# A decoder block on one core: the forget gate's two small products, both blocks of positions at a time

## The chip, the core and the metric

The kernel runs on one core of a Trainium2 chip. A core has TensorE (PE in the rows of the profile; its weight loads are shown as PEld), VectorE (DVE), ScalarE (ACT), GpSimd (POOL) and SyncE (SP), which here issues all DMA transfers. Each engine works through its own queue of instructions in order, and semaphores order the engines among each other. Matmul results go to PSUM, which has 8 banks; a bank holds 128 partitions of 512 float32 values. The metric is device time in microseconds (us) of one execution; several runs are given, and their median.

## The reference

One layer on 2048 positions of width 1024: an RMS norm, one input projection whose columns feed two token mixers (gated linear attention in chunks, and a short gated convolution), an output projection with residual, a SwiGLU feed-forward part with residual, and a last norm. All in float32. What the change touches is the forget gate of the attention, a product with a narrow matrix of rank 16 and a second product that widens it again:

```python
h = rmsnorm(x, norm1_g[l])
proj = h @ w_in[l]
p_q, p_k, p_v, p_g, p_a, c_b, c_c, c_h = jnp.split(proj, splits, axis=-1)   # p_a: 16 columns
gate_logits = (p_a @ w_gate_up[l] + b_gate[l]).astype(jnp.float32)          # 16 -> 256
log_a = (jax.nn.log_sigmoid(gate_logits) / GATE_NORMALIZER).reshape(bsz, seq, GLA_HEADS, GLA_DK)
o = gla_chunked(q, k, v, log_a)     # needs cumulative sums of log_a inside each chunk
```

## The kernel before

Features lie on partitions and positions along the free axis: a tile is 128 features by 512 positions (`PB`). The 2048 positions are four blocks of 512, worked on as two halves of two blocks. Every large product is made with operands split into a high and a low part (`split`: ScalarE copies the high part, VectorE subtracts to get the low part), three matmuls for each step of 128 (lines 328 to 330 in `product_step`: high·high, high·low, low·high).

A large product of a half is a `unit`: a 2 x 2 block product (two halves of the contraction, two blocks of positions) made with seven block products instead of four. The seven operands on the side of the positions are `B11` (features 0 to 511, first block), `B21` (features 512 to 1023, first block), `B22` (features 512 to 1023, second block) and the combinations `T1` = B12 - B11, `T2` = B22 - T1, `T3` = B22 - B12 and `T4` = B21 - T2 (the last made from T2 in place). `B12` itself, the second block's features 0 to 511, isn't kept as a full set of seven; it is `B11` + `T1`. Each operand is a list of four slices of 128 features, each with a high and a low part. For the first half `build_first` makes them on the fly: GpSimd subtracts (line 288), ScalarE and VectorE split (lines 146 and 147); the first unit's products run meanwhile. For the second half they were made earlier (`h1_ahead`), stored to DRAM and loaded back. On the other side, `unit_weights` makes seven combinations of a loaded weight tile (`raw`) on GpSimd (lines 311 to 318) and splits them into `wq`.

`in_proj` runs twelve units for a half and stores q, k, v and the output gate to DRAM scratch. Smaller jobs run beside it: they are Python generators in the list `background`, and after each block product `tick` lets the foremost one advance to its next `yield`: at every block product while `hurry` is set (from the start until the jobs up to `unhurried` are through), at every second one later. In the first half the list holds `gate_weights`, `gate(0)`, two `row_stats` jobs (squares of the third and fourth blocks: the `xn` steps at line 397), and `h1_ahead`; in the second half it holds `gate(1)`. `gla_half`, the chunked attention, is appended in each `in_proj`. The order of a program's instructions in each engine's queue is not the order in which the Python code emits them: when the kernel is built, a scheduler with its own estimate of durations places every instruction, so that a changed piece also moves others past each other. That order can be listed for a built program; it is called the built order below.

The forget gate of a half is `gate(half, ops)`. Its first product, `a_ps` (line 497), multiplies the rank-16 weights `wa_sb` with the operands. For the first block the operands are B11 and B21, for the second B11, T1 and B22. Each operand slice is streamed twice, its high and its low part, 512 columns a time. `wa_sb` holds, for each of 8 slices of features, 32 columns of high and 32 of low parts of the weights (of the 32, 16 are zero), so that the 64 lower partitions of the result hold the high and the low product; a matmul takes 128 columns of `wa_sb`, and the other 64 partitions of the result are not used. That makes 16 matmuls for the first block and 24 for the second, 80 over both halves. ScalarE copies the bank to `a_sb` (line 503), and the second product, z (line 513), contracts over those 64 partitions with `wgu_sb`, in float32, one matmul for each block and each 128 of the 256 gate features (`i`): four per half. Behind each z stand, in `forget_gate`, the steps of the decay: Abs, Exp and Ln on ScalarE (lines 518, 520, 521), add and subtract on VectorE (519, 522), four cumulative sums over 128 positions on VectorE (525), small exponentials `em` and `el` (528, 530), a subtraction (529), a product `dn` (531) and a store to DRAM scratch `sd`, which the attention loads later (`gla_load`; its product `kq` with exponentials of what was stored is at line 612, and the first matmul on it, `sc`, at 622).

Of the kernel before, what the change touches and what calls it, by code (L numbers as in the profile page):

```python
# [10 lines left out]
F32 = mybir.dt.float32  # L11
# [7 lines left out]
P = 128  # L19
# [28 lines left out]
def tile_hymba_block(ctx, tc, x, xt, win, wa, wgu, wout, wffn, wdown, wdown_first, small, out):  # L48
# [40 lines left out]
    dve.memset(scores[:], 0.0)  # L89
    carry = mixer.tile([P, HEADS, P], F32, name="carry")  # L90
# [43 lines left out]
    def bt(name, shape=(P, PB)):  # L134
        return bx[0].tile(list(shape), F32, name=name, tag="b")
# [9 lines left out]
    def split(src, hi, lo):  # L145
        last_hi[:] = [act.activation(hi, src, AF.Copy)]  # L146
        return dve.tensor_tensor(lo, src, hi.bitcast(F32), ALU.subtract)  # L147
# [339 lines left out]
    def gate(half, ops):  # L487


        for j, names in enumerate((("B11", "B21"), ("B11", "T1", "B22"))):  # L490
            a = bank("a_ps")
            for i, n in enumerate(names):
                k0 = 4 if n in ("B21", "B22") else 0
                for k in range(4):
                    w = wa_sb[:, (k0 + k) * 64 : (k0 + k) * 64 + P]
                    for e in range(2):
                        pe.matmul(
                            a[:], w, ops[n][k][:, e, :], start=(i, k, e) == (0, 0, 0),
                            stop=i == len(names) - 1 and k == 3 and e == 1,
                            skip_group_check=True,  # L500
                        )
# [5 lines left out]
    def forget_gate(b, a_sb):  # L507
        em, dn, el = [
            mtiny.tile([P, 2, PT], F32, name=n, tag=n, bufs=4) for n in ("em", "dn", "el")
        ]  # L510
        for i in range(2):
            z = bank("z")
            pe.matmul(
                z[:], wgu_sb[0:64, i * P : (i + 1) * P], a_sb[0:64, :], start=True, stop=True
            )
            bg = col(C_BG + i)
            t1, t2 = bt("g1"), bt("g2")
            act.activation(t1[:], z[:], AF.Abs, bias=bg)
            dve.tensor_scalar(t2[:], z[:], bg, 0.0, ALU.add, ALU.min)
            act.activation(t1[:], t1[:], AF.Exp, scale=-1.0)  # L520
            act.activation(t1[:], t1[:], AF.Ln, bias=one_t)
            dve.tensor_tensor(t2[:], t2[:], t1[:], ALU.subtract)
            for t in range(PT):
                s = slice(t * P, (t + 1) * P)
                dve.tensor_tensor_scan(t1[:, s], ones[:], t2[:, s], 0.0, ALU.mult, ALU.add)
            bs = t1.rearrange("p (a b) -> p a b", b=P)
            dd = t2.rearrange("p (a b) -> p a b", b=P)
            act.activation(em[:, i, :], bs[:, :, 63], AF.Exp, scale=1.0 / 16.0)
            dve.tensor_tensor(dd, bs, bs[:, :, 63:64].to_broadcast([P, PT, P]), ALU.subtract)
            act.activation(el[:, i, :], dd[:, :, P - 1], AF.Exp, scale=1.0 / 16.0)  # L530
            dve.tensor_tensor(dn[:, i, :], em[:, i, :], el[:, i, :], ALU.mult)
            store(s_d[b][i][:], t2[:])
            yield
        decays[b] = em, dn, el

    def in_proj(half, ops, first):
        def units():
# [103 lines left out]
    def gla_outputs(b, t, kq, kt, v, g):  # L641
# [7 lines left out]
        if b < NB - 1 or t < PT - 1:  # L649
            kv = ps.tile([P, 2, P], F32, name="kv", tag="mm")  # L650
            for i in range(2):
                for e in range(2):
                    pe.matmul(
                        kv[64 * e : 64 * e + 64, i, :], kt[:, i, 64 * e : 64 * e + 64],
                        v[:, 2 * i + e, :], start=True, stop=True,
                    )
            for i in range(2):
                last = el[:, i, t : t + 1]
                if first:
                    dve.tensor_scalar(state[i][:], kv[:, i, :], last, None, ALU.mult)  # L660
                else:
                    kvs = mtiny.tile([P, P], F32, name="kvs", tag="kvs")
                    dve.tensor_scalar(kvs[:], kv[:, i, :], last, None, ALU.mult)
# [437 lines left out]
```

## Time and profile before

Three runs: median 2149.33 us, from 2143.01 to 2150.7. The profiled execution took 2146.09 us, and its span is 2144.2 us.

| | busy us | share of the span | instructions |
|---|---|---|---|
| TensorE | 2043.6 | 95% | 9133 |
| VectorE | 1452.5 | 68% | 2034 |
| ScalarE | 1012.1 | 47% | 1962 |
| GpSimd | 997.0 | 46% | 714 |

The profile gives, for each engine, its instructions with start and duration, what an instruction waited for, and groups of like instructions (by line, engine and tile: `a_ps<-op,wa_sb` is an instruction that writes `a_ps` and reads `op` and `wa_sb`; x80 is their number; 128*128 128x512 at a matmul is the weights' and the moving operand's size). A timeline row begins with the start in us from the span's start and the duration in us; in square brackets stands how long the engine was idle before it, and what ended that. In a table of stretches a row has the stretch, then the sum and for PE, PEld, DVE, ACT and POOL the busy time (and number of instructions), then the granted TensorE clock as a share of full speed, the share of the DMA engines and GB/s. In a row of waits stand the total in us, how often, and the longest. A matmul in float32 is shown as two records, one in the split form as one. Matmuls overlap: each begins before the one ahead has ended, so the time that one costs is the distance between starts, not its duration.

### The profile page before, as it was taken

How to read it: one execution, taken by the hardware profiler on the slowest of the kernel's cores; microseconds unless marked ns; L12 is line 12 of the kernel's file. 1: busy time of each engine (PE TensorE's matmuls, PEld its weight loads, DVE VectorE, ACT ScalarE, POOL GpSimd, SP SyncE). 2: the span in 40 equal slices, each digit the busy share in tenths (PEclk: the TensorE clock that was granted, in tenths of full speed). 3: DMA queues.
4: the chain of work that ended last, by engine and by line, in shares of the span. 5: the costliest groups of instructions: out<-in, count | busy, mean ns of one | idle time of the engine just before them, and what ended most of it. 6: DMA issues, size and time to landing. Idle time of an engine off the chain costs nothing.

```text
span 2144.2 us, 26906 instructions
## 1 busy us (share of the span) xinstructions
PE 2043.6 (95%) x9133; PEld 1651.3 (77%) x9133; DVE 1452.5 (68%) x2034; ACT 1012.1 (47%) x1962; POOL 997.0 (46%) x714
## 2 busy tenths in 40 slices
PE   4899899999999999999999999999999999999996
PEld 2677687887888887788888887787888888887775
DVE  8849965556774486888887664554686677664554
ACT  4555434574544235555454553333454454553344
POOL 4526422122201274655655436774644654445774
PEclk9999999999999999999999999999999999999998
DMA  4259658532577884465464577689455455487662
GB/s 150 76 199 315 218 228 286 156 125 79 166 247 256 309 294 152 167 240 220 172 237 182 185 303 283 254 336 355 157 191 205 154 197 196 172 329 293 266 265 108
DMA packets 189977, 467.64 MB, mean 218 GB/s; under 512 B 19856, under 2 KB 65168, under 8 KB 180112
## 3 DMA queue, kind: packets, MB, share of 16 engines
q1 hardware_dynamic: 189840, 465.93, 59.9%
q8 instruction: 72, 1.18, 0.2%
q14 instruction: 65, 0.53, 0.1%
HBM read 297.03 MB, written 168.82 MB: 217 GB/s over the span
## 4 chain that ended last, share of the span: by engine, by line
PE 70%; DVE 11%; DMA 8%; issue 4%; ACT 3%; POOL 3%; SPq 1%; DVEq 0%; POOLq 0%; ACTq 0%
PE mm L328 20%; PE mm L330 20%; PE mm L329 19%; DVE wq L147 3%; PE mm L722 3%; PE mm L725 3%; PE mm L723 3%; DMA raw<-in_wdown_dram 2%; DVE h L440 2%; DMA raw<-in_wffn_dram 1%; DVE so L147 1%; DVE op L147 1%; DMA op<-shT 1%; DVE c L352 1%; ACT wq L146 1%
## 5 line engine op out<-in xcount | busy, mean ns | idle before, releaser
L328 PE MATMUL mm<-op,wq 128*128 128x512 f32 x2495 | 982.1, 395 | 33.0 <-ACT c L348 20.3
L330 PE MATMUL mm<-op,wq 128*128 128x512 f32 x2495 | 967.6, 392 | 12.4 <-DVE wq L147 11.2
L329 PE MATMUL mm<-op,wq 128*128 128x512 f32 x2495 | 975.6, 391 | 2.5 <-DVE op L147 2.5
L147 DVE TENSOR_TENSOR wq<-raw,wq 128x512 fp32r<-128x512 f32 (+2 forms) x628 | 536.6, 860 | 320.2 <-ACT wq L146 318.3
L146 ACT ACTIVATE wq<-raw 128x512 fp32r<-128x512 f32 (+2 forms) x628 | 367.1, 589 | 566.7 <-PE mm L330 415.4
L328 PEld LDWEIGHTS mm<-op,wq 128*128 128x128 f32 x2495 | 470.4, 189 | 152.1 <-ACT c L348 27.1
L330 PEld LDWEIGHTS mm<-op,wq 128*128 128x128 f32 x2495 | 470.5, 189 | 121.9 <-DVE wq L147 22.4
L329 PEld LDWEIGHTS mm<-op,wq 128*128 128x128 f32 x2495 | 470.7, 189 | 99.8 <-DVE op L147 3.0
L313 POOL TENSOR_TENSOR raw<-s,raw 128x512 f32<-128x512 f32 (+2 forms) x98 | 130.7, 1333 | 437.7 <-DVE wq L147 403.1
L352 DVE TENSOR_TENSOR c<-mm,c 128x512 f32<-128x512 f32 x270 | 185.1, 686 | 100.1 <-PE mm L330 98.0
L311 POOL TENSOR_TENSOR s<-raw 128x512 f32<-128x512 f32 (+2 forms) x98 | 130.8, 1335 | 207.9 <-DMA raw<-in_wffn_dram 96.1
L318 POOL TENSOR_TENSOR raw<-raw 128x512 f32<-128x512 f32 (+2 forms) x98 | 130.4, 1331 | 129.5 <-DVE wq L147 128.9
L348 ACT ACTIVATE c<-mm 128x512 f32<-128x512 f32 x270 | 156.4, 585 | 23.8 <-PE mm L330 23.0
L704 POOL TENSOR_TENSOR ssx<-ssx,q 128x512 f32<-128x512 f32 x52 | 75.2, 1459 | 151.0 <-ACT q L703 151.0
L312 POOL TENSOR_TENSOR raw<-raw 128x512 f32<-128x512 f32 (+2 forms) x98 | 137.2, 1400 | 4.6
L884 POOL TENSOR_TENSOR y<-c,y 128x512 f32<-128x512 f32 x66 | 98.6, 1496 | 67.3 <-DVE c L352 67.2
L147 DVE TENSOR_TENSOR so<-t,so 128x512 fp32r<-128x512 f32 x100 | 89.6, 902 | 23.8 <-ACT so L146 23.6
L722 PE MATMUL mm<-op,wq 128*128 128x512 f32 x256 | 100.9, 394 | 0.0
L723 PE MATMUL mm<-op,wq 128*128 128x512 f32 x256 | 99.7, 390 | 0.0
L146 ACT ACTIVATE wq<-s 128x512 fp32r<-128x512 f32 (+2 forms) x98 | 57.6, 588 | 89.2 <-PE mm L330 86.6
L147 DVE TENSOR_TENSOR wq<-s,wq 128x512 fp32r<-128x512 f32 (+2 forms) x98 | 81.9, 835 | 15.6 <-ACT wq L146 15.2
L146 ACT ACTIVATE so<-t 128x512 fp32r<-128x512 f32 x100 | 62.9, 630 | 48.6 <-DMA sa_B<-so 19.9
(177 smaller groups left out, 1931.2 us busy)
## 6 DMA issues: line engine op xcount, KB each, us to landing
raw<-in_wffn_dram SPq DMA_DIRECT2D x44, 1024.0 KB, 6.1
sa_T<-so SPq DMA_DIRECT2D x88, 512.0 KB, 4.9
op<-sa_T SPq DMA_DIRECT2D x88, 512.0 KB, 9.6
sa_B<-so SPq DMA_DIRECT2D x69, 512.0 KB, 3.4
op<-sa_B SPq DMA_DIRECT2D x69, 512.0 KB, 9.2
raw<-in_win_dram SPq DMA_DIRECT2D x24, 1024.0 KB, 5.7
raw<-in_wdown_dram SPq DMA_DIRECT2D x24, 768.0 KB, 6.1
sx<-y SPq DMA_DIRECT2D x48, 256.0 KB, 3.4
```

The lines of the kernel that those rows point to most:

```text
L146: last_hi[:] = [act.activation(hi, src, AF.Copy)]
L147: return dve.tensor_tensor(lo, src, hi.bitcast(F32), ALU.subtract)
L311: pool.tensor_tensor(s1, a21, a22, ALU.add)
L312: pool.tensor_tensor(a21, a11, a21, ALU.subtract)
L313: pool.tensor_tensor(a11, s1, a11, ALU.subtract)
L328: pe.matmul(o[:], wh, xh, start=first and k == 0, stop=False, skip_group_check=True)
L329: pe.matmul(o[:], wh, xl, start=False, stop=False, skip_group_check=True)
L330: return pe.matmul(o[:], wl, xh, start=False, stop=k == n - 1, skip_group_check=True)
L348: act.activation(t[:], o[:], AF.Copy)
L352: dve.tensor_tensor(t[:], o[:], t[:], ALU.add)
L722: pe.matmul(o[e, j][:], wh, m[:, 0, :], start=k == 0, stop=False)
L723: pe.matmul(o[e, j][:], wh, m[:, 1, :], start=False, stop=False)
```

## The change

The first product makes both blocks of positions in one bank. `wa_sb` is laid out anew: for each slice of features there are zeros and one or two copies of the high and low weights, 16 columns each, so that a window of 128 columns, begun at the right place, puts an operand's product into partitions 0 to 31 (first block), 32 to 63 (second block), or both (B11). B11, T1, B21 and B22 are streamed once each: 32 matmuls per half, 64 in all. One copy to `a_sb` per half takes the place of two. `gate_weights` splits three times (128 x 4 x 16 each) instead of once (128 x 8 x 32), and the whole of `wa_sb` is set to zero first.

The second product contracts over 32 rows per block: rows 0 to 31 for the first, 32 to 63 for the second. The two blocks' matmuls for one `i` are emitted one after the other into two banks, and the decay steps follow for both blocks. Four z matmuls per half stay, now in two pairs; their order changes from block by block to `i` by `i`. `wgu_sb` has 64 rows: the same 16 rows of weights four times, loaded with four transfers instead of one of 128 rows. `gate` now yields five times per half instead of six. The tile `kvs` of the attention has one buffer instead of two. In the built order the queues differ from before from this place to the end of the attention's second half; from there on they are the same.

```diff
-    wgu_sb = mixer.tile([P, 256], F32, name="wgu_sb")
-    wa_sb = mixer.tile([P, (KD + 1) * 64], F32R, name="wa_sb")
-    dve.memset(wa_sb[:, KD * 64 :].bitcast(F32), 0.0)
+    wgu_sb = mixer.tile([64, 256], F32, name="wgu_sb")
+    wa_sb = mixer.tile([P, 23 * 32], F32R, name="wa_sb")
+    dve.memset(wa_sb[:].bitcast(F32), 0.0)
...
     def gate_weights():
         raw = bt("wa", (P, KD, 32))
         load(raw[:], wa)
-        w = wa_sb[:, 0 : KD * 64].rearrange("p (k e c) -> p k e c", e=2, c=32)
-        split(raw[:], w[:, :, 0, :], w[:, :, 1, :])
+        top = wa_sb[:, 0 : 12 * 32].rearrange("p (k e c) -> p k e c", e=6, c=16)
+        low = wa_sb[:, 12 * 32 : 20 * 32].rearrange("p (k e c) -> p k e c", e=4, c=16)
+        r0, r1 = raw[:, 0:4, 0:16], raw[:, 4:8, 0:16]
+        split(r0, top[:, :, 2, :], top[:, :, 3, :])
+        split(r0, top[:, :, 4, :], top[:, :, 5, :])
+        split(r1, low[:, :, 2, :], low[:, :, 3, :])
         yield
...
     def gate(half, ops):
-        for j, names in enumerate((("B11", "B21"), ("B11", "T1", "B22"))):
-            a = bank("a_ps")
-            for i, n in enumerate(names):
-                k0 = 4 if n in ("B21", "B22") else 0
-                for k in range(4):
-                    w = wa_sb[:, (k0 + k) * 64 : (k0 + k) * 64 + P]
-                    for e in range(2):
-                        pe.matmul(
-                            a[:], w, ops[n][k][:, e, :], start=(i, k, e) == (0, 0, 0),
...
-            a_sb = bt("a_sb")
-            act.activation(a_sb[:], a[:], AF.Copy)
-            yield
-            yield from forget_gate(2 * half + j, a_sb)
+        a = bank("a_ps")
+        names = "B11", "T1", "B21", "B22"
+        for n in names:
+            for k in range(4):
+                q = {"B11": 3 * k + 1, "T1": 3 * k, "B21": 2 * k + 13, "B22": 2 * k + 12}[n]
+                w = wa_sb[:, 32 * q : 32 * q + P]
+                for e in range(2):
+                    pe.matmul(
+                        a[:], w, ops[n][k][:, e, :], start=(n, k, e) == ("B11", 0, 0),
+                        stop=n == "B22" and k == 3 and e == 1, skip_group_check=True,
+                    )
+        a_sb = bt("a_sb")
+        act.activation(a_sb[:], a[:], AF.Copy)
+        yield
...
         for i in range(2):
-            z = bank("z")
-            pe.matmul(
-                z[:], wgu_sb[0:64, i * P : (i + 1) * P], a_sb[0:64, :], start=True, stop=True
-            )
...
+            zs = [bank("z") for _ in range(2)]
+            for j in range(2):
+                r = slice(32 * j, 32 * j + 32)
+                pe.matmul(
+                    zs[j][:], wgu_sb[r, i * P : (i + 1) * P], a_sb[r, :], start=True, stop=True
+                )
+            for j in range(2):
+                forget_gate(2 * half + j, i, zs[j], *small[j])
+                yield
...
-                    kvs = mtiny.tile([P, P], F32, name="kvs", tag="kvs")
+                    kvs = mtiny.tile([P, P], F32, name="kvs", tag="kvs", bufs=1)
...
-    load(wgu_sb[:], wgu)
+    for i in range(4):
+        load(wgu_sb[16 * i : 16 * i + 16, :], wgu[0:16, :])
```

The new `forget_gate(b, i, z, em, dn, el)` holds the steps behind one z unchanged.

More of the change, by code (lines that the diff above doesn't have):

```diff
@@ L507, in forget_gate @@
[L507 to L510, printed above, removed]
-        for i in range(2):
-            z = bank("z")
-            pe.matmul(
-                z[:], wgu_sb[0:64, i * P : (i + 1) * P], a_sb[0:64, :], start=True, stop=True
[L515 to L534, printed above, removed]
@@ new lines, in gate @@
+        a_sb = bt("a_sb")
+        act.activation(a_sb[:], a[:], AF.Copy)
+        yield
+        small = {}
+        for j in range(2):
+            small[j] = decays[2 * half + j] = [
+                mtiny.tile([P, 2, PT], F32, name=n, tag=n, bufs=4) for n in ("em", "dn", "el")
+            ]
+        for i in range(2):
+            zs = [bank("z") for _ in range(2)]
[4 more added lines that the diff above has]
+                )
+            for j in range(2):
+                forget_gate(2 * half + j, i, zs[j], *small[j])
+                yield
@@ new lines, in forget_gate @@
+    def forget_gate(b, i, z, em, dn, el):
+        bg = col(C_BG + i)
+        t1, t2 = bt("g1"), bt("g2")
+        act.activation(t1[:], z[:], AF.Abs, bias=bg)
+        dve.tensor_scalar(t2[:], z[:], bg, 0.0, ALU.add, ALU.min)
+        act.activation(t1[:], t1[:], AF.Exp, scale=-1.0)
+        act.activation(t1[:], t1[:], AF.Ln, bias=one_t)
+        dve.tensor_tensor(t2[:], t2[:], t1[:], ALU.subtract)
+        for t in range(PT):
+            s = slice(t * P, (t + 1) * P)
+            dve.tensor_tensor_scan(t1[:, s], ones[:], t2[:, s], 0.0, ALU.mult, ALU.add)
+        bs = t1.rearrange("p (a b) -> p a b", b=P)
+        dd = t2.rearrange("p (a b) -> p a b", b=P)
+        act.activation(em[:, i, :], bs[:, :, 63], AF.Exp, scale=1.0 / 16.0)
+        dve.tensor_tensor(dd, bs, bs[:, :, 63:64].to_broadcast([P, PT, P]), ALU.subtract)
+        act.activation(el[:, i, :], dd[:, :, P - 1], AF.Exp, scale=1.0 / 16.0)
+        dve.tensor_tensor(dn[:, i, :], em[:, i, :], el[:, i, :], ALU.mult)
+        store(s_d[b][i][:], t2[:])
```

2 lines of the change are left out of this document (removed).

## The prediction

> **What bounds the kernel now.** I read the page's shares and slices first, then the waits of TensorE, then its timeline around the gate's instructions.
>
> ```profile
> PE   4899899999999999999999999999999999999996
> PEclk9999999999999999999999999999999999999998
> PE mm L328 <- ACT c L348: 20.3, 15, 4.4
> PE mm L330 <- DVE wq L147: 11.2, 6, 3.2
> 400.00:500.00 100.00, 100.00 (x514) 80.87 (x513) 54.48 (x102) 62.29 (x132) 21.82 (x16) 1.00 0.39 123
> ```
>
> TensorE is busy in nearly all slices; between 400 and 500 us it never rests, so there a removed matmul is worth its full time. Early on it does wait: mostly for ScalarE copies that free a bank, then for VectorE splits of weights. The gate of the first half lies in that early stretch, the gate of the second half in the saturated one. The same saving is therefore worth different amounts in the two places.
>
> **The change, part by part.**
>
> ```profile
> L497 PE MATMUL a_ps<-op,wa_sb x80: 387/396/628, 74.2 to 509.7; 128*128 128x512 f32 x80
> L513 PE MATMUL z<-a_sb,wgu_sb x16: 589/589/693, 80.8 to 522.7; 64*128 64x512 f32 x16
> 80.52 0.40 PE L330 MATMUL mm<-op,wq 128*128 128x512 f32 x1
> 80.85 1.12 PE L513 MATMUL z<-a_sb,wgu_sb 64*128 64x512 f32 x2
> 81.90 0.50 PE L328 MATMUL mm<-op,wq 128*128 128x512 f32 x1
> 82.24 0.40 PE L329 MATMUL mm<-op,wq 128*128 128x512 f32 x1
> 82.47 0.39 PE L330 MATMUL mm<-op,wq 128*128 128x512 f32 x1
> 96.50 1.98 PE L513 MATMUL z<-a_sb,wgu_sb 64*128 64x512 f32 x4
> 98.41 0.50 PE L328 MATMUL mm<-op,wq 128*128 128x512 f32 x1
> ```
>
> *First product.* 80 matmuls become 2 x 32 = 64. Matmuls overlap, so their price is the distance of starts, 82.47 - 82.24 = 0.23 us: 16 x 0.23 = 3.7 us, 1.8 per half.
>
> *Second product.* Each of the 8 z matmuls shows as two records. A lone one holds TensorE from 80.85 to 81.90, 1.05 us; two in a row take 98.41 - 96.50 = 1.91, so a second adds 0.86. Each switch between the 128-row matmuls and these costs about 0.1 on either side (80.85 - 80.52 and 82.24 - 81.90, less 0.23), 0.2 in all. In the built order before, six stand alone and two together (two alone in the first half, all four in the second): 6 x 1.05 + 1.91 + 7 x 0.2 = 9.6 us. After the change four pairs stand together. No row shows a 32-row matmul. Bounds: a second matmul that is free (pair 1.05) and one that overlaps nothing (1.91). The nearest rows are the 64-row `sc` matmuls, which also alternate between two groups of rows:
>
> ```profile
> 535.12 0.71 PE L622 MATMUL sc<-kq 64*128 64x128 f32 x8 [1.88 <-DVE kq L612]
> 541.84 0.39 PE L646 MATMUL o_ps<-vt,scores 128*128 128x128 f32 x2
> ```
>
> Two full-height records of this width end 0.39 after the first starts and one takes 0.275, so starts are 0.11 apart; eight in a line would put the last start 0.8 after the first, while `sc` shows 0.71 - 0.27 = 0.44, four distances instead of seven. That is what follows if the first record of one matmul overlaps the second record of the matmul ahead, and nothing more. Two matmuls of two records then take three slots of four: 1.05 + 0.43 = 1.48. Four pairs: 4 x 1.48 + 4 x 0.2 = 6.7 us; saving 2.9 (bounds 1.2 and 4.6), of it 1.25 in the first half and 1.65 in the second.
>
> The Trainium skill, "TensorE: Matmul & The Clock Gate", Part 3, says that matmuls in different row groups start about 4 ns apart, so that a pack costs one matmul. By it a pair would take 1.05 and the four would save 1.7 us more. The `sc` row agrees only in part; it shows overlap, but four distances and not three.
>
> *First half, where it stands.* TensorE is in order, so what stands behind a waiting matmul waits too. In the built order the whole first product now comes early: 12 of the 32 at the place of the old 16, and all 32, which need T1 of all four slices, ahead of the `A12`·`B21` product and of every z. Before, that product and two z filled the time in which T1 and T2 came. These rows time the operands:
>
> ```profile
> 74.21 5.32 PE L497 MATMUL a_ps<-op,wa_sb 128*128 128x512 f32 x16
> 82.58 1.68 POOL L288 TENSOR_TENSOR t<-h,t 128x512 f32<-128x512 f32 x1 [1.47 <-DVE op L147]
> 84.29 1.15 ACT L146 ACTIVATE op<-t 128x512 fp32r<-128x512 f32 x2 [0.76 <-POOL t L288]
> 101.26 0.39 PE L328 MATMUL mm<-op,wq 128*128 128x512 f32 x1
> 114.20 0.50 PE L328 MATMUL mm<-op,wq 128*128 128x512 f32 x1 [1.87 <-ACT c L348]
> 135.94 0.80 PE L328 MATMUL mm<-op,wq 128*128 128x512 f32 x1 [3.00 <-ACT c L348]
> ```
>
> T1's last split stands behind that of T4 on ScalarE, which waits for GpSimd until 84.3: it is ready at 85.4 (84.29 + 1.15). VectorE's low part follows some 0.7 later, so TensorE has its 32 gate matmuls and 12 others done at about 86.2 + 19 x 0.23 = 90.5, that is 44 x 0.23 = 10 us of work in 16.3 us: 6.3 us idle where there was none. From there to the next unit stand 39 matmuls and two pairs: 90.5 + 9.0 + 2 x 1.68 = 102.9, against 101.26 before. An idle stretch has a second price:
>
> ```profile
> 116.00:118.00 2.00, 2.00 (x6) 1.57 (x5) 0.67 (x3) 0.00 (x0) 0.00 (x0) 0.50 0.73 197
> 236.00:238.00 2.00, 1.77 (x8) 1.47 (x9) 2.00 (x4) 1.26 (x3) 1.62 (x1) 1.00 0.93 353
> ```
>
> After the wait that ended at 114.20 the granted clock was 0.50; after a longer one at 236 it stayed 1.00. A slow spell of some 3 us loses half, 1.5 us. I count 1.3: 104.2. The Trainium skill (the same page, Part 1) puts the slowdown behind an idle window of about 3.4 us; the 1.87 us wait shows it can come sooner, and by the page alone this 1.3 would be left out.
>
> *VectorE's share.* The four blocks of gate work after z are only moved, but now start after all operand splits:
>
> ```profile
> L525 DVE TENSOR_TENSOR_SCAN g<-ones,g x32: 392/398/1458, 89.7 to 532.2; 128x128 f32<-128x128 f32 x32
> L519 DVE TENSOR_SCALAR g<-z,sml x8: 736/740/752, 83.0 to 526.5; 128x512 f32<-128x512 f32 x8
> L522 DVE TENSOR_TENSOR g<-g,g x8: 662/676/683, 86.8 to 528.5; 128x512 f32<-128x512 f32 x8
> L529 DVE TENSOR_TENSOR g<-g x8: 679/683/694, 92.2 to 535.6; 128x512 f32<-128x512 f32 x8
> 112.45 0.21 ACT L151 ACTIVATE rl<-msq 128x4 f32<-128x4 f32 x1 [0.71 <-DVE msq L401]
> ```
>
> A block is 0.74 + 0.68 + 4 x 0.40 + 0.68 = 3.7 us, four 15. Before, about half was done by 96; after, the first can start at the first z pair, about 95.6. So the em and el steps that ScalarE runs in order come later too, and the bank copies stand behind them: the copy that ended the wait at 114.20 was itself behind `rl`, which waited for VectorE; after, it stands behind the last `em` and lands near 117. I take 3 us late at that place (from 1 to 8). The wait of 135.94 shrinks to about 1.9: in the built order only two `xn` squares, not four, stand ahead of that copy, which leaves three ScalarE steps of 0.6. The first half: +3.0 - 1.1 = +2 us (from -8, if the saved 3.1 count in full and both waits go, to +8). From 140 to 400 the order is shuffled, with 10 to 12 us of waits to win or lose; nothing favours a sign: 0, within 3.
>
> *Second half.* TensorE is full: -1.8 - 1.65 = -3.5. The wait of 1.88 at 535.12 came because the decay blocks of the last z, 36 matmuls ahead, sat in front of `kq` on VectorE; in the built order 67 matmuls, 15 us, lie between. I count it gone: -5.4 (from -2.5 to -7.5).
>
> *At nothing.*
>
> ```profile
> 14.30 0.33 SPq L138 DMA_DIRECT2D wgu_sb<-in_wgu_dram  x1
> 14.98 2.17 SPq L138 DMA_DIRECT2D raw<-in_win_dram  x2
> raw<-in_win_dram SPq DMA_DIRECT2D x2, 1024.0 KB, 7.2
> 24.67 1.72 POOL L311 TENSOR_TENSOR s<-raw 128x512 f32<-128x512 f32 x1
> 74.64 0.63 ACT L146 ACTIVATE op<-t 128x512 fp32r<-128x512 f32 x1 [4.51 <-POOL t L288]
> 1.47 0.48 DVE L89 MEMSET scores<- 128x512 f32 x1
> L663 DVE TENSOR_SCALAR kvs<-kv,el x28: 341/344/351, 335.4 to 670.9; 128x128 f32<-128x128 f32 x28
> ```
>
> Three more loads are 3 x 0.33 = 1.0 us of SP ahead of the `raw` loads; the first lands at 14.98 + 7.2 = 22.2 and is used at 24.67, when GpSimd's own work lets it: 1.5 us of cover stay (bare, it costs 1.0). Two more small splits of `wa_sb` fall into ScalarE's idle 4.51. The longer memset is under 0.8 us of a VectorE that waits for loads. One `kvs` buffer orders only VectorE's own steps, which are in order.
>
> **The sum.** +2 + 0 - 5.4 = -3.4 us: 2142.7 for the profiled execution's 2146.1. The median of runs lies 3.2 above that execution; from the median I get 2149.3 - 3.4 = 2146.
>
> **The rivals.**
>
> 1. *All of it counts.* TensorE bounds throughout: -3.7 - 2.9, and the waits at 114, 136 and 535 (1.9, 3.0, 1.9) go: -13 us, 2136. For it: the saturated window. Against: the late T1 and the decay blocks.
> 2. *Slower: VectorE's decay blocks as one heap.* Its place is the stretch from 95 to 140 us: 15 us in a row hold up weight splits and bank copies of the next two units. Price up to 8 us there, and each long wait can add a slow spell of 1.5; with two, +11 - 1.1 - 5.4 = +5, 2154. It decides from 6.5 us lost at the place of 114.20 (6.5 = 1.1 + 5.4), where it eats the second half's gain. For it: VectorE ran without a pause in that stretch already.
> 3. *Pairs do not overlap.* The second product then saves 1.2 for 2.9: -1.7 us in all, 2148. Against it: `sc`.
> 4. *Pairs overlap fully*, as the page's rule has it: 1.05 for a pair, -5.1 in all, 2144.
>
> **How the numbers follow.** Forecast 0.5, rival 1 0.15, rival 2 0.15, rival 3 0.1, rival 4 0.1. The runs before spread over 7.7 us (0.36%), so about 0.5%, 10.7 us, is what can be told from no change. Only rival 1 reaches faster by that: most of its chance, 0.12. Rival 2 passes it only with further waits in the shuffled 140 to 400: 0.1. The rest, 0.78, is same. Range: rival 1's 2136 to rival 2's 2154, widened by 1 to 2 us for the shuffled stretch: 2135 to 2156.
>
> **What would show it.** `a_ps` x64 and z pairs of about 1.5 us from start to next matmul (1.05: rival 4; 1.9: rival 3). TensorE idle about 6 us between 77 and 87; the unit's first matmul that stood at 101.26 at 103 to 104; the wait of 114.20 ending near 117; no wait before the first `sc` of the second half. Wrong if TensorE shows no idle there (rival 1), if the wait ends past 120 (rival 2), or if the stretch from 140 to 400 moves by more than 3 us.

## The result, and the profile after

The changed kernel takes 2152.45 us (median of 15 runs, 2150.23 to 2156.72), the kernel before in the same runs 2148.7 us (15 runs, 2143.01 to 2151.51). The ratio is 1.0023, with a 95% interval from 1.0014 to 1.0032: slower by 0.23%, 4.9 us (the two medians lie 3.75 apart), where 3.4 us less was forecast. That lies in the range and inside the 0.5% called "no change", but on the other side. The execution profiled after the change took 2154.2 us, its span is 2152.3 us.

Of the changed kernel: the slices of TensorE and of its granted clock, then rows of TensorE's waits (total us, times, longest), then two groups of instructions (busy us, mean ns | idle before).

```profile
PE   4788999999999999999999999999999999999996
PEclk9899999999999999999999999999999999999998
```

```profile
PE mm L328 <- ACT c L348: 22.2, 15, 4.3
PE mm L330 <- DVE wq L147: 9.9, 10, 3.2
PE rb_ps L407 <- DVE rep L406: 4.6, 1, 4.6
PE mm L328 <- ACT op L146: 3.9, 3, 2.2
```

```profile
L504 PE MATMUL a_ps<-op,wa_sb 128*128 128x512 f32 x64 | 19.1, 453 | 0.0
L520 PE MATMUL z<-a_sb,wgu_sb 32*128 32x512 f32 x16 | 4.5, 640 | 0.0
```

The 16 matmuls are gone as counted. The second to fourth slice (54 to 215 us), 8, 9 and 9 before, are 7, 8 and 8 now; the fifth is 9 for 8. There is a wait that the kernel before does not have, 4.6 us for `rep` (a copy of row statistics that the transposes `rb_ps` read), and the waits for splits of the operands (`op`) are 3.9 us in place of 0.5.

The same stretches of 20 us in both kernels (sum and PE, PEld, DVE, ACT, POOL busy, granted clock, DMA share, GB/s). The kernel before:

```profile
80.00:100.00 20.00, 20.00 (x76) 13.53 (x76) 17.00 (x29) 13.81 (x28) 8.32 (x5) 1.00 0.18 67
100.00:120.00 20.00, 18.13 (x73) 14.44 (x72) 14.92 (x32) 13.24 (x36) 4.29 (x3) 0.91 0.73 252
140.00:160.00 20.00, 20.00 (x91) 16.29 (x90) 10.39 (x19) 7.69 (x15) 5.62 (x4) 1.00 0.58 188
200.00:220.00 20.00, 18.88 (x82) 15.05 (x81) 19.90 (x21) 10.44 (x19) 13.09 (x8) 1.00 0.89 312
```

The changed kernel:

```profile
80.00:100.00 20.00, 16.97 (x62) 11.41 (x63) 9.25 (x14) 10.66 (x19) 6.96 (x5) 0.91 0.15 44
100.00:120.00 20.00, 16.60 (x70) 12.32 (x67) 19.27 (x41) 15.06 (x42) 4.01 (x3) 0.99 0.63 219
140.00:160.00 20.00, 16.15 (x66) 13.09 (x67) 9.15 (x19) 7.37 (x18) 4.21 (x3) 0.91 0.45 159
200.00:220.00 20.00, 16.16 (x58) 12.46 (x57) 15.66 (x20) 10.65 (x19) 11.11 (x7) 0.83 0.89 313
```

TensorE loses 3 us between 80 and 100, 1.5 in the next stretch, nearly 4 between 140 and 160, and 2.7 between 200 and 220, there with a clock of 0.83. VectorE's decay steps have moved from the first stretch (17.0 to 9.3) to the second (14.9 to 19.3), as the prediction had it.

TensorE's timeline of the changed kernel, at the places that the prediction names and at some that it doesn't:

```profile
81.77 0.51 PE L328 MATMUL mm<-op,wq 128*128 128x512 f32 x1 [0.63 <-ACT op L146]
85.41 0.60 PE L328 MATMUL mm<-op,wq 128*128 128x512 f32 x1 [2.17 <-ACT op L146]
95.54 1.13 PE L520 MATMUL z<-a_sb,wgu_sb 32*128 32x512 f32 x4
96.59 0.50 PE L328 MATMUL mm<-op,wq 128*128 128x512 f32 x1
118.49 0.51 PE L328 MATMUL mm<-op,wq 128*128 128x512 f32 x1 [2.75 <-ACT c L348]
136.24 0.50 PE L328 MATMUL mm<-op,wq 128*128 128x512 f32 x1 [1.69 <-ACT c L348]
143.85 0.48 PE L407 MATMUL rb_ps<-ident,rep 128*128 128x128 f32 x1 [4.59 <-DVE rep L406]
143.98 0.77 PE L328 MATMUL mm<-op,wq 128*128 128x512 f32 x1
212.86 0.80 PE L328 MATMUL mm<-op,wq 128*128 128x512 f32 x1 [2.92 <-ACT c L348]
518.89 0.50 PE L330 MATMUL mm<-op,wq 128*128 128x512 f32 x1 [1.25 <-DVE wq L147]
525.71 0.71 PE L632 MATMUL sc<-kq 64*128 64x128 f32 x8
```

T1's slice ends a wait at 85.41, the matmul that waited at 114.20 waits until 118.49, and the first `sc` of the second half waits for nothing. By the count of matmuls, the one that waited 3.00 us at 135.94 is now the one at 143.98, directly behind a transpose that waits 4.59; the wait of 1.69 at 136.24 belongs to a matmul 12 places ahead of it, which waited for nothing before. New are also the 2.92 at 212.86 (0.36 before) and the 1.25 at 518.89.

The forecast idle time between 77 and 87 is there only by half: 0.63 at 81.77, 0.22 at 82.50 and 2.17 at 85.41, 3.0 us where 6.3 were forecast. The 44 matmuls that were counted for that stretch take 14.8 us instead of 10 (74.24 to 92.04, less the idle 3.0), since the clock is slow on both sides of the waits:

```profile
76.00:78.00 2.00, 2.00 (x6) 1.60 (x5) 0.56 (x1) 0.27 (x1) 1.67 (x1) 0.50 0.00 0
86.00:88.00 2.00, 2.00 (x6) 1.49 (x5) 0.16 (x1) 0.52 (x1) 1.27 (x1) 0.50 0.00 0
```

To see where time goes, I take the start of the n-th matmul of the large products (`mm<-op,wq`) in each trace and subtract the kernel before's; a positive number is a lag in us. The columns are places in the profiled execution of the kernel before. The kernels are those of the next section; the first row is another execution of the kernel before itself.

| | 99 | 149 | 207 | 408 | 517 | 708 | 819 | 897 | 2062 |
|---|---|---|---|---|---|---|---|---|---|
| before_again | 0.0 | -0.8 | -1.3 | -2.6 | -2.6 | -3.1 | -3.1 | +1.9 | +3.2 |
| after | +2.2 | +8.3 | +14.9 | +10.3 | +7.4 | +5.2 | +5.2 | +7.1 | +7.6 |
| half1_only | +3.4 | +7.1 | +10.6 | +6.2 | +6.2 | +8.9 | +8.9 | +12.9 | +10.0 |
| half2_only | +0.2 | +0.2 | -0.3 | -2.1 | -4.8 | -5.6 | -5.6 | -0.8 | +2.2 |
| t1_last | -1.2 | +3.4 | +8.6 | +3.8 | +0.9 | -1.3 | -1.3 | -2.0 | +1.6 |
| t1_last_yield | -1.9 | -3.3 | -3.6 | -3.6 | -6.3 | -4.6 | -4.6 | +0.8 | -0.4 |
| extra_yield | -1.8 | -3.5 | +0.2 | +0.8 | -1.9 | -1.9 | -1.9 | +2.7 | +3.6 |
| z_by_block | +0.4 | -3.7 | -3.7 | -3.7 | -4.2 | -7.6 | -7.6 | -3.3 | -5.3 |

The lag of the changed kernel grows to 8 us by 149 and 15 by 207, and falls in the rest of the first half and in the second, to 5.2. A large part of the fall has one place: the kernel before waits there ahead of an `sc` of the attention, the changed kernel doesn't, and its lag falls from 12.8 to 8.4 across that place. The kernel before:

```profile
347.42 1.23 PE L622 MATMUL sc<-kq 64*128 64x128 f32 x8 [3.72 <-issue]
```

The first row is the measure of the others: two executions of one kernel differ by 3.1 us one way at 708 and by 3.2 the other way at the end.

### The profile page after: what moved, and what is told of

Read it like the earlier page. It is cut to its first block, busy times and chain, and to the rows that moved or that the text cites. A ratio compares the mean times of both kernels' runs of the same rounds, so it can differ in the third digit from the quotient of the medians.

```text
span 2152.3 us, 26908 instructions
## 1 busy us (share of the span) xinstructions
PE 2048.4 (95%) x9117; PEld 1652.2 (77%) x9117; DVE 1454.0 (68%) x2036; ACT 1011.0 (47%) x1962; POOL 996.5 (46%) x714
## 4 chain that ended last, share of the span: by engine, by line
PE 75%; DMA 9%; DVE 9%; ACT 3%; issue 2%; POOL 1%; SPq 1%; DVEq 0%; ACTq 0%; POOLq 0%
PE mm L328 21%; PE mm L330 21%; PE mm L329 21%; PE mm L732 2%; PE mm L733 2%; PE mm L735 2%; DVE wq L147 2%; DMA raw<-in_wdown_dram 1%; DVE h L440 1%; DMA op<-sa_T 1%; DMA raw<-in_win_dram 1%; DMA op<-sa_B 1%; DVE so L147 1%; DVE op L147 1%; DMA h<-in_xt_dram 1%
```

## The experiments

Each is measured against the kernel before on the same chip, and the runs are from several chips; so where two of them are compared, the ratios decide. A ratio is good to about 0.1%, the difference of two of them to about 0.15%, 3 us. Unless it is said otherwise, an edit is shown against the changed kernel.

| kernel | median us (runs) | ratio to before | 95% interval |
|---|---|---|---|
| changed kernel | 2152.45 (15) | 1.0023 | 1.0014 to 1.0032 |
| half2_only | 2147.82 (11) | 1.0005 | 0.9994 to 1.0016 |
| half1_only | 2159.93 (5) | 1.0056 | 1.0042 to 1.0071 |
| apart | 2151.42 (12) | 1.0018 | 1.0006 to 1.0029 |
| apart_again (the same kernel) | 2151.34 (11) | 1.0016 | 1.0004 to 1.0028 |
| apart_kvs2 | 2146.51 (11) | 0.9998 | 0.9986 to 1.0009 |
| kvs_one | 2149.63 (11) | 1.0008 | 0.9999 to 1.0018 |
| after_kvs2 | 2154.01 (12) | 1.0034 | 1.0023 to 1.0044 |
| t1_last | 2148.01 (11) | 1.0006 | 0.9996 to 1.0017 |
| extra_yield | 2150.64 (12) | 1.0018 | 1.0006 to 1.0031 |
| t1_last_yield | 2146.48 (11) | 0.9996 | 0.9986 to 1.0007 |
| z_order_alone | 2150.10 (12) | 1.0015 | 1.0003 to 1.0028 |
| z_by_block | 2143.29 (11) | 0.9982 | 0.9970 to 0.9994 |
| z_by_block_kvs2 | 2142.99 (11) | 0.9984 | 0.9971 to 0.9997 |
| before_again (the kernel before) | 2147.94 (12) | 0.9999 | 0.9988 to 1.0010 |

**One half at a time.** The products stay block by block in one of the halves, with the new layout of the weights (`gate_apart`, which uses rows 0 to 31 or 32 to 63 of one bank per block and one z at a time, as before); the other half is merged.

```diff
# half2_only
-        [gate_weights(), gate(0, ops), row_stats(2), row_stats(3), unhurried(), h1_ahead()]
+        [gate_weights(), gate_apart(0, ops), row_stats(2), row_stats(3), unhurried(), h1_ahead()]
# half1_only
-    background.append(gate(1, ops))
+    background.append(gate_apart(1, ops))
```

> The merged form in the second half only; the first half keeps two products and lone second products (on the new layout of the weights), and its queues stand as before the change. Theory (the loss is made in the first half, the second half gains): the second half's saving counts in full, 1.8 us for 8 matmuls and 2 x 1.05 us for the two paired z, and perhaps the 1.9 us wait ahead of the first sc; 4 to 5 us faster than before, about 2144. Rival (the new layout, the 32-row matmuls or the single kvs buffer cost something wherever they stand): no faster than before, 2149 or more.

> The merged form in the first half only; up to the second half the queues are those of the changed kernel. Theory: the whole loss, without the second half's gain: 3.75 + 4 to 5 = 8 to 9 us slower than before, about 2157. Rival (the loss is spread over both halves): 2 to 4 us slower, 2151 to 2153.

With the second half alone merged the time is that of before, with the first alone it is 12 us longer. The first loses and the second doesn't, but the loss is larger than was expected and the gain of 4 to 5 us is missing. In the trace, half2_only is level with before to 207 and leads by 5.6 us at 708; before_again, which has none of the change, leads by 3.1 there. One part of the missing gain can be seen: the wait before the first `sc` of the second half, which the forecast counted as gone, is still there in half2_only.

```profile
519.92 0.71 PE L660 MATMUL sc<-kq 64*128 64x128 f32 x8 [2.49 <-DVE kq L650]
```

**Neither half merged.** Both edits together: what is left of the change is the layout, the loads, the three splits, 32 rows for a z, and one buffer for `kvs`.

> Neither half merged: the first products stay apart (16 and 24 matmuls), the second products stand alone as before; but the weights have the new layout, their loads and splits are the new ones, the second product contracts over 32 rows, and kvs has one buffer. TensorE's queue differs from before in fewer than ten places. Theory: these side edits cost nothing, within 1.5 us of before, and the loss measured with the first half merged is the merging's own. Rival: the side edits carry a part of the loss (half1_only at +12 us and half2_only at 0 would add up to the changed kernel's +4 to 5 if the side edits alone cost about 8).

3.3 to 4 us more than before instead of nothing, and the same again when it was measured once more. So half2_only saves 0.11 to 0.13% against apart, 2.4 to 2.8 us, which by itself is not clear of nothing; the changed kernel saves 0.33% against half1_only, 7 us. The first half merged costs 0.18% (changed kernel against half2_only) to 0.4% (half1_only against apart), 4 to 8.5 us. What a half costs or saves depends on which form the other has: each moves others past each other in the built order.

**Where T1 stands.** T1's matmuls go behind all others in the first product.

```diff
-        names = "B11", "T1", "B21", "B22"
+        names = "B11", "B21", "B22", "T1"
...
-                        stop=n == "B22" and k == 3 and e == 1, skip_group_check=True,
+                        stop=n == "T1" and k == 3 and e == 1, skip_group_check=True,
```

> The changed kernel with the operands of the first product summed in the order B11, B21, B22, T1. Only the place of the 32 first products in TensorE's queue moves; the queues behind 120 us stay those of the changed kernel. Theory A (the early T1 makes TensorE wait, and that lateness stays): the waits of 0.6, 0.2 and 2.2 us between 81 and 86 go, and the slow clock with them, 3 to 4 us faster than the changed kernel, about 2149. Rival B (the loss is made behind 120 us, by the row statistics that come one step earlier): within 1 us of the changed kernel, 2152.

2148.0: 4.4 us less by the medians, 3.7 by the ratios, and the waits at 81 to 86 us are gone (the lag at 99 falls from +2.2 to -1.2). The wait for `rep` stays. TensorE's timeline of t1_last:

```profile
137.73 0.48 PE L407 MATMUL rb_ps<-ident,rep 128*128 128x128 f32 x1 [4.23 <-DVE rep L406]
```

**The lost yield.** `gate` yields five times instead of six, so that the `row_stats` jobs behind it start one block product earlier. One more yield puts them back.

```diff
         act.activation(a_sb[:], a[:], AF.Copy)
         yield
+        yield
```

> The changed kernel, order B11, T1, B21, B22 kept, with one more yield in the gate, six as before. Theory B (the step lost brings the row statistics' transposes one block product too early into TensorE's queue): the wait of 4.6 us on the rep copies near 144 us goes, 2 to 4 us faster than the changed kernel, 2148 to 2150. Theory A (only the early T1 matters): as the changed kernel, 2152. By both, t1_last_yield stays the faster of the two.

> The same order B11, B21, B22, T1, and one more yield in the gate, so that it gives six again: the jobs behind it start at the block product at which they started before the change, and the queues behind 100 us stand nearly as before. Theory A and B together (early T1, and the step lost): the first half saves its 3 us at least in part and the second half 4 to 5, 2141 to 2145, faster than before. A alone: as t1_last, 2149. B alone: about 2148. Rival C (the saved matmuls are worth nothing, since other engines set the pace): 2149 in every case.

With the yield alone it is 2150.6 (1.0018), where 2148 to 2150 or 2152 had been expected: this is not clear of the changed kernel. With both edits the time is that of before, 2146.5 (0.9996), and clear of the changed kernel; 2141 to 2145 had been expected of it. The chain behind the wait of 143.85 can be read in the changed kernel's queues. First SyncE, ScalarE and VectorE of the changed kernel:

```profile
132.39 2.87 SPq L138 DMA_DIRECT2D xn<-in_x_dram  x6
139.17 0.63 ACT L397 ACTIVATE xn<-xn 128x512 f32<-128x512 f32 x1 [1.23 <-DMA xn<-in_x_dram]
141.85 0.16 DVE L400 TENSOR_TENSOR msq<-ssq 128x4 f32<-128x4 f32 x1 [5.42 <-ACT xn L397]
143.57 0.36 DVE L406 COPY rep<-msq 128x128 f32<-128x128 f32 x2
```

The same in the kernel before:

```profile
128.45 4.17 SPq L138 DMA_DIRECT2D xn<-in_x_dram  x6
139.37 0.16 DVE L400 TENSOR_TENSOR msq<-ssq 128x4 f32<-128x4 f32 x1 [1.63 <-ACT xn L397]
143.63 0.35 DVE L406 COPY rep<-msq 128x128 f32<-128x128 f32 x2
145.56 0.27 PE L407 MATMUL rb_ps<-ident,rep 128*128 128x128 f32 x1
```

`rep` is written at 143.6 in both. But the loads of `xn` go out 4 us later in the changed kernel, which is the lag that it has by then (4.3 us at 118.49), and its transposes `rb_ps` stand 36 large matmuls, 8 us, earlier in TensorE's queue. So TensorE waits for statistics that before were ready 1.6 us ahead of their use, and everything queued behind waits too. In t1_last, where the early lag is gone, the wait is still 4.23: it is the place of the transposes that makes it. In the kernel with both edits the transpose stands without a wait:

```profile
142.25 0.27 PE L407 MATMUL rb_ps<-ident,rep 128*128 128x128 f32 x1
```

By the ratios the extra yield gives 1.1 us beside T1 second and 2.1 beside T1 last, neither clear of nothing; the place of T1 gives 3.7 to 4.7 us, both clear. In the traces the yield looks larger (a lag of +0.2 for +14.9 at 207): the changed kernel's profiled execution has a slow stretch at 200 to 220 that I can't put down to the yield alone. Nor does extra_yield test the yield alone. It is 4 us ahead of the changed kernel at 99 already, so the built order of the first product moved too; and it goes from 3.2 us ahead of before to 2.2 behind it between 172 and 185, with the clock at 0.50 from 178 to 182, behind a wait that the changed kernel does not have:

```profile
175.37 0.50 PE L330 MATMUL mm<-op,wq 128*128 128x512 f32 x1 [1.87 <-DVE wq L147]
```

**The order of z.** T1 last, the extra yield, and the second products block by block, so that adjacent ones use the same rows.

```diff
-        for i in range(2):
-            zs = [bank("z") for _ in range(2)]
-            for j in range(2):
-                r = slice(32 * j, 32 * j + 32)
+        for j in range(2):
+            r = slice(32 * j, 32 * j + 32)
+            for i in range(2):
+                z = bank("z")
                 pe.matmul(
-                    zs[j][:], wgu_sb[r, i * P : (i + 1) * P], a_sb[r, :], start=True, stop=True
+                    z[:], wgu_sb[r, i * P : (i + 1) * P], a_sb[r, :], start=True, stop=True
                 )
-            for j in range(2):
-                forget_gate(2 * half + j, i, zs[j], *small[j])
+                forget_gate(2 * half + j, i, z, *small[j])
                 yield
```

> t1_last_yield with the second products block by block: two matmuls that stand next to each other use the same 32 rows, so none can overlap. In the first half the queues are the same otherwise. The trace of the changed kernel shows a pair of different rows in about 1.06 us to the next matmul; if that is overlap, two of the same rows take 1.9 here, and the kernel is 0.86 x 4 = 3 to 4 us slower than t1_last_yield where TensorE is the bound, about 2150. Rival (a 32-row matmul is itself faster): 1.06 for two here too, and no change. If TensorE's saved time is hidden by waits: 1.9 us for two, but less than 1.5 us slower.

That fell: 2143.3 us, 0.18% below before, the interval clear of 1. Against t1_last_yield it is 0.14%, 3.0 us, less, which is at the edge of what two ratios can tell; the 3 to 4 us more that had been expected are excluded. What was expected of TensorE itself did come. Its timeline:

```profile
93.40 1.98 PE L521 MATMUL z<-a_sb,wgu_sb 32*128 32x512 f32 x4
95.31 0.50 PE L328 MATMUL mm<-op,wq 128*128 128x512 f32 x1
```

Two z in the same rows hold TensorE for 95.31 - 93.40 = 1.91 us; a pair in different rows, in the changed kernel, for 96.59 - 95.54 = 1.05. The overlap is worth 0.86 us a pair, and the version without it is not the slower one. In the traces the two are level at 149, 207 and 408 (0.1 to 0.4 apart). At 517, behind the second half's pairs, z_by_block is 2.1 us behind, as two pairs of 0.86 make it; at 708 it is 3.0 ahead. The turn has one place. TensorE of t1_last_yield waits there for the copy of a bank, and the clock behind it is 0.50; in z_by_block the first matmul behind the same group (`kv`) starts without a wait. First two rows of t1_last_yield, then one of z_by_block:

```profile
555.93 0.80 PE L328 MATMUL mm<-op,wq 128*128 128x512 f32 x1 [2.46 <-ACT c L348]
556.00:558.00 2.00, 2.00 (x5) 1.63 (x6) 2.00 (x4) 1.75 (x7) 0.16 (x1) 0.50 0.72 271
```

```profile
554.51 0.50 PE L328 MATMUL mm<-op,wq 128*128 128x512 f32 x1
```

Between 550 and 570 t1_last_yield loses 4.3 us to z_by_block by this. The same edit on the changed kernel alone:

> The changed kernel with the second products block by block, T1 second and no more yields. If the order of z is worth its 3 us by itself (decay steps of the first block end earlier, less is queued behind them): about 2149. If it is worth something only where the rest of the first half keeps its place: 2152, as the changed kernel. If pairing gains its 0.86 us for each pair on the path: 2155.

2150.1 us, 1.0015 against 1.0023: the intervals overlap, so this only points the same way. The expectation named decay steps of the first block that end earlier as the reason. No run shows that: the wait that makes the difference in the traces ends 37 us after the last decay step of t1_last_yield (518.2). Why the copy is late there stays open.

**The one buffer of `kvs`.** The difference of apart left 3.5 us unexplained. Alone in the kernel before:

```diff
-                    kvs = mtiny.tile([P, P], F32, name="kvs", tag="kvs")
+                    kvs = mtiny.tile([P, P], F32, name="kvs", tag="kvs", bufs=1)
```

> The kernel before with one buffer for kvs and nothing else of the change. The kernel with neither half merged took 0.18% (3 to 4 us) more than before, and its queues are those of this kernel apart from five instructions. Theory (the one buffer costs this, by the new order of the attention's steps): about 3.5 us more than before, 2151.5. Rival (the cost came from the new weights' layout, loads and splits, or from slow stretches of the clock that fell on those runs): within 1 us of before.

And taken back (`kvs2`), which needs room: windows of 64 instead of 128 columns of `wa_sb`, with as many matmuls (its two parts also change places, and the copy to `a_sb` takes 64 partitions).

```diff
-    wa_sb = mixer.tile([P, 23 * 32], F32R, name="wa_sb")
+    wa_sb = mixer.tile([P, 20 * 32], F32R, name="wa_sb")
...
-                w = wa_sb[:, 32 * q : 32 * q + P]
+                w = wa_sb[:, 32 * q : 32 * q + 64]
...
-                    kvs = mtiny.tile([P, P], F32, name="kvs", tag="kvs", bufs=1)
+                    kvs = mtiny.tile([P, P], F32, name="kvs", tag="kvs")
```

> The changed kernel with two buffers for kvs, as before. The room comes from the layout of the gate's weights: windows of 64 columns instead of 128, 20 groups of 32 columns instead of 23, with the same number of matmuls. Theory (the one buffer costs some 3.5 us): about 2149, no slower than before. Rival (the buffer costs nothing): 2152.5 as the changed kernel.

> The kernel with T1 last, one more yield and z block by block, with two buffers for kvs and windows of 64 columns of the gate's weights. Theory (the one buffer costs some 3.5 us): about 2140, 0.4% less than before. Rival: 2143.3, as with one buffer.

> Neither half merged, two buffers for kvs, windows of 64 columns of the gate's weights: the queues are those of the kernel before apart from the new weights' layout, loads and splits and the rows of z. With one buffer and windows of 128 columns the same took 3.3 to 4 us more than before. Theory S (these side edits cost it): again about 3.5 us more than before. Theory B (the one buffer costs about half of it, as its run alone with 1.7 us hints): 1 to 2 us. Theory N (both are the scatter of slow stretches of the clock): within 1 us of before.

> The kernel with neither half merged once more, beside the one above. Theory S and B: 3 to 4 us more than before, as the first time. Theory N: nearer to before than the first time, within 1.5 us.

> The kernel before itself, measured like the others: how far a comparison of this kind comes from nothing. All theories: within 1 us of before. If it differs by 2 us or more, differences of 3 us between such comparisons say nothing.

The kernel before against itself gives 0.9999, and apart gives its 3.5 us a second time. With two buffers apart is level with before (0.9998): its layout, loads, splits and rows of z cost nothing that can be measured, and the one buffer is left, unless the narrower windows save something. One buffer alone in the kernel before gives 1.7 us, with an interval from nothing to 3.9. But in the changed kernel and in z_by_block two buffers gain nothing (2154.0 and 2143.0). So the buffer costs some 2 to 4 us where the rest of the order is that of before, each figure with 2 to 3 us of uncertainty, and none that shows in another order.

A part of it has a place. TensorE's timeline around 630 us, first of before_again:

```profile
629.43 0.71 PE L622 MATMUL sc<-kq 64*128 64x128 f32 x8
630.08 0.50 PE L725 MATMUL mm<-op,wq 128*128 128x512 f32 x1
```

Then of kvs_one:

```profile
630.52 0.71 PE L622 MATMUL sc<-kq 64*128 64x128 f32 x4
631.16 0.50 PE L722 MATMUL mm<-op,wq 128*128 128x512 f32 x1
...
632.98 0.71 PE L622 MATMUL sc<-kq 64*128 64x128 f32 x4
633.62 0.44 PE L628 MATMUL kt_ps<-ident,kq 128*128 128x128 f32 x2
```

With one buffer the built order splits a group of eight `sc` records into two of four, in this trace and in both of apart, and each four hold TensorE as long as the eight: 0.64 and 0.65 us. With the switch between tile heights (0.2) that is some 0.85 us, and the lag of all three grows by 0.8 around that place. With two buffers the group is whole in apart_kvs2. It is split in z_by_block too and whole in z_by_block_kvs2, where the times don't tell the two apart: 0.85 us is less than these runs resolve. Where the rest lies, single executions don't show.

## Why the prediction was wrong

*First product, second product.* x64 as counted. A pair stands 1.05 us from start to the next matmul, not 1.48: that is rival 4, the rule of the Trainium skill ("TensorE: Matmul & The Clock Gate", Part 3) that matmuls in different row groups run at once. The trace agrees with it here. The term was mis-sized by a wrong reading of `sc`: I took its four distances for a partial overlap, but the rows around 630 us show that four of its records alone hold TensorE as long as all eight (0.64 and 0.65), so the other four cost nothing there either. By itself that would have made the forecast 1.7 us shorter, and z_by_block shows that the overlap doesn't decide the time.

*The first half, up to the wait of 114.20.* Most of the mechanism was right: T1 ended its wait at 85.41 (forecast 85.4), the unit's first matmul, by the count of matmuls, stood at 103.4 (103 to 104), and the wait of 114.20 ended at 118.49 (117, from 1 to 8 us late allowed). But TensorE was idle for 3.0 us, not 6.3. I had priced the 44 matmuls of that stretch at 0.23 us, 10 us, though the row at 74.21 shows 16 of them in 5.32 us, some 0.33 each; they took 14.8. The product was done at 92.04 instead of 90.5, and the two pairs then took 0.9 us less than forecast; that 103.4 fits so well is in part luck, two errors against each other. t1_last shows that the early T1 is worth 3.7 to 4.7 us.

*"The wait of 135.94 shrinks to about 1.9 ... +3.0 - 1.1 = +2": this step failed.* Between the places of 114.20 and 140 the changed kernel doesn't win 1.1 us, it loses 3.9 (lag 4.3, then 8.2). The matmul that waited 3.00 at 135.94 now stands behind a transpose that waits 4.59, and another matmul 12 places ahead waits 1.69. I should have found it: one yield fewer moves `row_stats` and its transposes up, and the step that moved was never followed to what it needs. The lost yield is told of in the section on the change; the prediction has no term for it. Instead of +2 the merged first half costs 4 to 8.5 us.

*"From 140 to 400 the order is shuffled ... 0, within 3."* At its two ends this holds (8.2 at 140, 10.3 at 408, by single executions), but not because nothing happened: the lag rises to 14.9 at 207, with the wait of 212.86 and a slow clock behind it, and the wait of 3.72 at 347 that the changed kernel doesn't have gives 4.4 us back. That is luck more than foresight.

*"One kvs buffer orders only VectorE's own steps": this step failed too*, by about 3.5 us where neither half is merged. The figure is that of apart with one buffer against two, so the narrower windows of the second are in it. `kvs` is written and read by VectorE alone, as I said, but a buffer is also an input to the built order, which moved other engines' steps. In the changed kernel it can't be separated, since two buffers gained nothing there.

*Second half: sized too large for one order of the rest.* Of the 5.4 us, 2.4 to 2.8 arrive when half2_only is set against apart, 7 when the changed kernel is set against half1_only. The 1.9 us for the wait before `sc` hang on the order too: in half2_only it is still there, with 2.49; in the changed kernel it is gone, but a wait of 1.25 at 518.89 has come. That the saved time of a full stretch arrives in full was not shown.

*The sum.* Side edits 0, first half +2, second half -5.4 came out as +3.7, +3.9 and -2.6, taken one after the other from before over apart (1.0017, the mean of its two), half2_only (1.0005) and the changed kernel (1.0023), with differences of ratios times 2148.7. Each of the three carries 0.1 to 0.15% (2 to 3 us) of uncertainty from its two intervals. Over half1_only instead of half2_only the first half is +8.4 and the second -7.1, with the same sum. On both ways the side edits and the first half miss to the slow side; the second half misses to the slow side on one and to the fast side on the other. Rival 2's sign was right, but its condition, 6.5 us lost at the place of 114.20, was not met (4.3), and what came on top, at the end of its stretch, has another mechanism: not decay steps in a heap, but transposes queued too early.

*How the saved time is given back.* Between 819 and 897 the rows of the table move by -0.7 to +5.5 us, before_again by +5.0, though by the section on the change the queues there are the same in all. There TensorE waits for VectorE's splits, and what follows the wait differs between executions of the same kernel. Two executions of the kernel before: the wait in TensorE's timeline and what follows it (the clock is the third column from the right), first of the one shown at the beginning:

```profile
826.32 0.50 PE L330 MATMUL mm<-op,wq 128*128 128x512 f32 x1 [2.32 <-DVE wq L147]
```

```profile
826.00:828.00 2.00, 1.69 (x7) 1.42 (x8) 0.86 (x2) 0.00 (x0) 1.66 (x2) 1.00 0.00 0
```

Then of before_again:

```profile
823.95 0.50 PE L330 MATMUL mm<-op,wq 128*128 128x512 f32 x1 [3.06 <-DVE wq L147]
```

```profile
824.00:826.00 2.00, 2.00 (x6) 1.58 (x7) 0.50 (x1) 0.33 (x1) 2.00 (x2) 0.61 0.00 0
826.00:828.00 2.00, 2.00 (x7) 1.60 (x6) 1.08 (x1) 0.30 (x1) 0.88 (x1) 0.54 0.00 0
```

After the wait the clock stays at 1.00 in one and is 0.61 and 0.54 in the other, which loses 0.39 x 2 + 0.46 x 2 = 1.7 us, a part of the 5.0. So a lead of a few us in one trace is not yet a shorter run.

## What to carry to other kernels

A job that yields once less, or a buffer that is taken away, is an edit of the order of everything around it: list for each step that moves up in an in-order queue what it needs and when that is there, down to the loads, before pricing it at nothing. A row that is to size a new piece has to be read with its clock: here the large matmuls stand 0.43 us apart at a clock of 0.50 and 0.23 at 1.00, and the idle time that was counted on shrank by as much. A product that sums several operands should end with the one that comes last. Savings of a few us are compared over runs, with the kernel against itself beside them, and not by the time at which two single traces stand at some place.

The best version found (T1 last, the yield put back, second products block by block) takes 2143.3 us, 0.9982 of the kernel before (0.9970 to 0.9994).

## What the runs showed of the hardware

The slow clock behind a wait comes in some executions and not in others, at the same place with the same wait. After the wait of 1.87 us that ended at 114.20 the clock of the kernel before was 0.50 in the execution shown in the prediction. In before_again:

```profile
114.64 0.50 PE L328 MATMUL mm<-op,wq 128*128 128x512 f32 x1 [1.92 <-ACT c L348]
```

```profile
116.00:118.00 2.00, 2.00 (x11) 1.63 (x10) 1.11 (x5) 0.26 (x1) 0.00 (x0) 1.00 0.53 164
```

The Trainium skill (the same page, Part 1) has a window that runs free of the kernel, which fits that it is a matter of chance where a wait falls; that the clock drops behind a wait of 1.87 us differs from the idle window of 3.4 us that the Trainium skill names there, and here the measurement decides.

Two float32 matmuls of 32 rows in different rows of the array take 1.05 us, as long as a lone one (1.05 in apart, 82.05 to 83.10), where two in the same rows take 1.91. Four `sc` records alone take 0.64 us and eight together 0.65, so a group that the order splits in this way pays its price twice.
